# A hybrid attention and mLSTM block: ordered runs for the mLSTM's numerators, later scores, wider first values, and a convolution tap on ScalarE

## The chip, the cores and the metric

The kernel runs on one core of a Trainium2 chip. The metric is device time in microseconds of one execution: 1467.97 us before, the median of 3 runs (1467.61 to 1468.28).

## The reference, cut to what matters

The model has two layers over 512 tokens of width 1024: a dilated window attention and a SwiGLU, then an mLSTM and a SwiGLU, with RMS norms. The change lies in the mLSTM alone. For it the reference computes, with 8 heads, keys and queries of 64 and values of 128:

```
proj = xn @ w_in                      # q, k (512 + 512), v (1024), output gate (1024), gates (16)
qk   = silu(causal depthwise conv over 4 taps of the first 1024 columns, + bias)
dmat = cumsum(log f) differences + i, causal
sm   = exp(dmat - m_t) * (q @ k^T)
num  = sm @ v (+ the carried state);  den = sum of sm
h    = num / max(|den|, exp(-m_t));   h = rms_norm(h) * head_gain
out  = (h * sigmoid(o_pre)) @ w_out
```

The kernel doesn't carry a state between chunks of 64 tokens; it takes all 512 tokens at once, in blocks of 128 by 128 below the diagonal.

## The kernel before, in words

Products are made in split precision: every operand is split into a high and a low part of a rounded fp32 format, and three products (high by high, high by low, low by high: `SPLITS`) stand for one. Weights come in chunks of 128 x 1024 numbers (512 KB) on SyncE's (SP's) DMA queue, with three buffers; for each chunk ScalarE makes the high part (L207) and VectorE the low part (L208). So all projections are long rows of TensorE products, fed by the two other engines.

Two kinds of projection matter here. `project` (L238) has the weights stationary and 512 tokens moving, 512 columns in each product: q and k ("mqk"), the output gate ("mo"), the output projection ("mwo"). `project_tokens` (L270) has tokens stationary and weights moving, 256 columns in each product: the values ("mv"), because the numerators need them by token. `project_v(pr)` makes the values of two heads in two chunks of 48 products, and ScalarE copies them out of PSUM into `vaug` with a scale (L914).

**Ticks.** `advance()` is called after every chunk and counts one tick; `defer` and `at_tick` queue a function for a tick counted from the mLSTM's start. Ticks 1 to 4 follow the four chunks of `project_v(0)` and `project_v(1)`; after tick 2 come the gates (a long chain of small VectorE steps). Ticks 5 to 12 are the eight chunks of q and k (24 products each; the order of the four parts is 0, 2, 1, 3), 13 to 16 those of `project_v(2)` and `project_v(3)`, 17 to 24 those of the output gate. After each part of q and k, `convolve` makes two channels' tiles: VectorE multiplies the first tap (L899), adds three more (L901), and ScalarE applies Silu (L903).

**Per head.** `stack(p)` builds split keys and queries of two heads (L1033 to L1039). `weights(hh)` broadcasts a row into the PSUM tile "nb" (L1049), adds the causal mask (L1051), takes exponentials on ScalarE (L1057, L1060), makes the scores ("m0s" for head 0, L1062 and L1063, eight products in the two "s" banks), and multiplies both on VectorE (L1064). `numerators(hh)` makes ten fp32 products (twenty instructions, L1076) into two tiles of the two "o" banks, takes the denominators and norms (L1084 to L1094, with four squares on ScalarE, L1090), and writes the normalised head `yt` with four VectorE instructions (L1097), two from each bank. `outputs(hh)` transposes `yt` by four TensorE products (L281) in the single "t" bank, which "nb" uses too, and ScalarE copies the result to `y[hh]` (L1106). `HEAD_AT` gives each head its ticks for the three.

**Order.** A tick only sets where a function stands in the program's order. A scheduler then orders each engine's instructions by when it reckons them ready, with the program's order as priority; a TensorE product of a later chunk may overtake a numerator that isn't ready. The engines keep that order on the chip. Two helpers bind it: `run(*fns)` makes all TensorE instructions of the functions follow the last TensorE instruction of the program so far, and notes the run's last one; and a block under `fenced()`, which every projection uses, follows the last run. The attention uses `run` already; in the mLSTM nothing does.

PSUM has eight banks: three "acc", two "s", two "o" and one "t".

Of the kernel before, what the change touches and what calls it, by code (L numbers as in the profile page):

```python
# [11 lines left out]
F32 = mybir.dt.float32  # L12
F32R = mybir.dt.float32r
I32 = mybir.dt.int32
AF = mybir.ActivationFunctionType
ALU = mybir.AluOpType
AX = mybir.AxisListType
P = 128

SEQ = 512  # L20
D = 1024
KC = D // P
TB = SEQ // P
# [11 lines left out]
RUN_AT = (2, 3, 5, 10)  # L35
LAST_AT = (2, 4)
STACK_AT = (9, 11, 14, 16)
HEAD_AT = ((9, 11, 13), (10, 13, 15), (12, 15, 17), (13, 16, 18), (15, 18, 19), (16, 19, 21), (18, 21, 22), (19, 21, 23))
W_BUFS = 3
SPLITS = [(0, 0), (0, 1), (1, 0)]  # L40

# [28 lines left out]
def tile_hybrid_dilated_attn_mlstm(  # L70
# [4 lines left out]
    nc = tc.nc  # L75
# [53 lines left out]
    def col(key, i):  # L129
        return cols[:, row_of[key] + i:row_of[key] + i + 1]  # L130
# [10 lines left out]
    def advance():  # L141
        tick[0] += 1
        run_deferred(lambda t: t <= tick[0])
# [32 lines left out]
    def fenced():  # L176
        return tc.issue_after(fence[0]) if fence[0] is not None else nullcontext()
# [82 lines left out]
    def project_tokens(pairs, w2d, c0, evac, name, tok=lambda t, tb: t[:, tb * P:(tb + 1) * P]):  # L260

        acc = [acc_tile("%s_%d" % (name, m)) for m in range(2)]
        for ch in range(KC // 4):
            whl = split_chunk(weight_chunk(w2d, ch, c0, 4, "%s_k%d" % (name, ch)))
            for m in range(2):
                with fenced():
                    for i, k in itertools.product(range(2), range(4)):
                        kk = ch * 4 + k
                        for a, b in SPLITS:
                            nc.tensor.matmul(  # L270
                                acc[m][:, i * 256:(i + 1) * 256],
                                tok(pairs[a][kk], 2 * m + i), whl[b][:, k, :],
                                start=(kk == 0 and i == 0 and (a, b) == SPLITS[0]),
                                stop=(kk == KC - 1 and (a, b) == SPLITS[-1]),
                                skip_group_check=True)
                if ch == KC // 4 - 1:
                    evac(m, acc[m])
            advance()

    def transpose_into(dst_ps, i, src, n=P):  # L280
# [593 lines left out]
    with ExitStack() as mctx:  # L874
# [20 lines left out]
        def convolve(c):  # L895
            for m in range(2):
                j = 2 * c + m
                u = mp.tile([P, SEQ], F32, tag="conv", name="conv%d" % j, bufs=2)
                nc.vector.tensor_scalar(u, pre[m][:, 0:SEQ], col("convw", j), None, op0=ALU.mult)  # L899
                for w in range(1, 4):  # L900
                    nc.vector.scalar_tensor_tensor(u, pre[m][:, w:w + SEQ], col("convw", w * KC + j), u,  # L901
                                                   op0=ALU.mult, op1=ALU.add)
                nc.scalar.activation(qk[j], u, AF.Silu, bias=col("convb", j))  # L903
# [6 lines left out]
        def project_v(pr):  # L910
            def evac(m, acc):
                for i in range(2):
                    tb = 2 * m + i
                    nc.scalar.activation(  # L914
                        vaug[:, tb, 2 * pr:2 * pr + 2, 0:P],
                        acc[:, i * 256:(i + 1) * 256].rearrange("p (h d) -> p h d", h=2),
                        AF.Copy, scale=rtok[:, tb:tb + 1])
            project_tokens(pair, w_in2, D + pr * 256, evac, "mv%d" % pr)
# [37 lines left out]
        mneg = mp.tile([P, SEQ], F32R, name="mneg")  # L956
        nc.gpsimd.memset(mneg.bitcast(F32), 0.0)
        base = tick[0]
        project_v(0)
        gates()  # L960
        hook()
        ve = nc.vector
# [39 lines left out]
        i = 0  # L1002
# [16 lines left out]
                nc.tensor.transpose(tp[:, i * H:(i + 1) * H], emn[:, b * P:(b + 1) * P], ident[:H, :H])  # L1019
            nc.vector.tensor_copy(bcol.rearrange("p a b -> p (a b)"), tp[:, :(npair + TB) * H])  # L1020

        project_v(1)

        stacks = {}

# [19 lines left out]
        def weights(hh):  # L1045
            nm = "m%d" % hh
            ks, qs, ql = stacks[hh]
            nb = ps.tile([P, 512], F32, tag="t", name=nm + "nb", bufs=1)
            nc.tensor.matmul(nb, sel[:, hh, :], mneg, start=True, stop=True)  # L1049
            tmp = mp.tile([P, TB, P], F32, tag="dtmp", name=nm + "d", bufs=2)  # L1050
            nc.vector.tensor_tensor(tmp, blk(nb), mask_causal_t.unsqueeze(1).to_broadcast([P, TB, P]), op=ALU.add)  # L1051
            sm = []
            for kb in range(TB):
                w = SEQ - kb * P
                e = mp.tile([P, w], F32, tag="e%d" % kb, name=nm + "e", bufs=2)
                bias = lambda qb: bcol[:, pidx[kb, qb], hh:hh + 1]
                nc.scalar.activation(e[:, :P], tmp[:, kb, :], AF.Exp, bias=bias(kb))  # L1057
                for qb in range(kb + 1, TB):
                    o = (qb - kb) * P
                    nc.scalar.activation(e[:, o:o + P], nb[:, qb * P:(qb + 1) * P], AF.Exp, bias=bias(qb))  # L1060
                sp = ps.tile([P, 512], F32, tag="s", name=nm + "s", bufs=2)
                nc.tensor.matmul(sp[:, :w], ks[:, kb * P:(kb + 1) * P], qs[:, kb * P:], start=True, stop=False)  # L1062
                nc.tensor.matmul(sp[:, :w], ks[:, kb * P:(kb + 1) * P], ql[:, kb * P:], start=False, stop=True)  # L1063
                nc.vector.scalar_tensor_tensor(e, sp[:, :w], 0.125, e, op0=ALU.mult, op1=ALU.mult)  # L1064
                sm.append(e)
            sms[hh] = sm

        def numerators(hh):
            nm = "m%d" % hh
            sm = sms[hh]  # L1070
            num = [ps.tile([P, 512], F32, tag="o", name=nm + "num", bufs=2) for _ in range(2)]
            nv = lambda qb: num[qb // 2][:, (qb % 2) * 256:(qb % 2) * 256 + P + 1]
            for qb in range(TB):
                for kb in range(qb + 1):
                    o = (qb - kb) * P
                    nc.tensor.matmul(nv(qb), sm[kb][:, o:o + P], vaug[:, kb, hh, :],  # L1076
                                     start=(kb == 0), stop=(kb == qb))

            rr = mp.tile([P, TB], F32, tag="rr", name=nm + "rr", bufs=2)
            aa = mp.tile([P, TB], F32, tag="aa", name=nm + "aa", bufs=2)  # L1080
            s2 = mp.tile([P, TB], F32, tag="s2", name=nm + "s2", bufs=2)
            for t in range(2):
                den = num[t].rearrange("p (a b) -> p a b", a=2)[:, :, P]
                nc.vector.tensor_copy(rr[:, 2 * t:2 * t + 2], den)  # L1084
            nc.vector.scalar_tensor_tensor(aa, rr, -1.0, rr, op0=ALU.mult, op1=ALU.max)
            nc.vector.tensor_tensor(aa, aa, bcol[:, npair:, hh], op=ALU.max)
            nc.vector.reciprocal(rr, aa)
            for qb in range(TB):
                junk = mp.tile([P, P], F32, tag="junk", name=nm + "j", bufs=2)
                nc.scalar.activation(junk, nv(qb)[:, :P], AF.Square, scale=rr[:, qb:qb + 1],  # L1090
                                     accum_out=s2[:, qb:qb + 1])
            nc.vector.tensor_scalar(s2, s2, 1.0 / P, EPS, op0=ALU.mult, op1=ALU.add)
            rq = rsqrt_newton(mp, s2, TB, nm + "rq")
            nc.vector.tensor_tensor(rr, rr, rq, op=ALU.mult)  # L1094
            yt = mp.tile([P, SEQ], F32, tag="yt", name=nm + "yt", bufs=2)
            for qb in range(TB):
                nc.vector.tensor_scalar(yt[:, qb * P:(qb + 1) * P], nv(qb)[:, :P], rr[:, qb:qb + 1], None,  # L1097
                                        op0=ALU.mult)
            yts[hh] = yt

        def outputs(hh):
            tp = ps.tile([P, 512], F32, tag="t", name="m%dyT" % hh, bufs=1)
            for qb in range(TB):
                transpose_into(tp, qb, yts[hh][:, qb * P:(qb + 1) * P])
            y[hh] = y_tile(hh, "y%d" % hh)
            nc.scalar.activation(y[hh], tp, AF.Copy)  # L1106

        def at_tick(t, fn):
            defer(base + t - tick[0], fn)
        at_tick(8, exponents)  # L1110
        for p, t in enumerate(STACK_AT):
            at_tick(t, lambda p=p: stack(p))
        for hh, (t0_, t1_, t2_) in enumerate(HEAD_AT):
            at_tick(t0_, lambda hh=hh: weights(hh))
            at_tick(t1_, lambda hh=hh: numerators(hh))
            at_tick(t2_, lambda hh=hh: outputs(hh))
        for c in (0, 2, 1, 3):
            project_qk(c)
            convolve(c)
# [6 lines left out]
        for c in range(KC // 2):  # L1126
            def evac(m, acc, c=c):
                j = 2 * c + m
                t = mp.tile([P, SEQ], F32, tag="conv", name="og%d" % j, bufs=2)
                nc.vector.tensor_tensor(t, acc, rbc, op=ALU.mult)  # L1130
                nc.scalar.activation(t, t, AF.Tanh, scale=0.5)
                nc.vector.scalar_tensor_tensor(y[j], t, 1.0, y[j], op0=ALU.add, op1=ALU.mult)
# [114 lines left out]
```

## Time and profile before

| | |
|---|---|
| median of 3 runs | 1467.97 us (1467.61 to 1468.28) |
| the profiled execution's own time | 1467.84 us |
| its span, from first to last instruction | 1466.1 us, granted TensorE clock 0.999 |
| busy: TensorE (PE), weight loads (PEld) | 1454.4 us, 1239.4 us |
| busy: VectorE (DVE), ScalarE (ACT), GpSimd (POOL) | 784.7 us, 528.5 us, 125.3 us |
| the mLSTM, first value product to first product of the output projection | 873.4 to 1050.1 us |

The profile is of one execution. A row of a timeline has the start in microseconds from the span's start, the length, the engine, the source line, the operation, the tiles written and read, and the shapes; a bracket tells how long the engine was idle before it and which instruction released it. Buffer numbers are left out of names, so "mv" stands for all value projections; "f1j" and "fin" are the last SwiGLU. Matmuls overlap in the pipeline: a 512-column product shows 0.39 us, though the next one starts earlier, so spacings are read from start to start.

### The profile page before, as it was taken

What the parts mean: (1) busy time and instruction counts of PE and PEld (TensorE: products, weight loads), DVE (VectorE), ACT (ScalarE), POOL (GpSimd) and SP (SyncE); (2) the same over time, 40 slices, a digit from 0 to 9 for tenths busy, and PEclk for the clock granted to TensorE, in tenths of its full rate; (3) what the DMA queues carried; (4) which work ended last, traced back from release to release, by engine and by line L of the source; (5) the groups of instructions that cost most, each with busy time, mean ns of one, the idle gap of its engine ahead of it and who ended that gap; (6) DMA issues with size and microseconds to landing.
All of it is one profiled execution on the core that took longest, in us unless ns stands there. A gap on an engine that the chain in (4) does not pass through costs nothing. (4 is left out here: it accounts for less than half of the span.)

```text
span 1466.1 us, 18728 instructions
## 1 busy us (share of the span) xinstructions
PE 1454.4 (99%) x7378; PEld 1239.4 (85%) x7378; DVE 784.7 (54%) x1523; ACT 528.5 (36%) x963; POOL 125.3 (9%) x135
## 2 busy tenths in 40 slices
PE   9999999999999999999999999999999999999998
PEld 7898888889888888888888889798888888888887
DVE  8747556556565554344333348987765344343233
ACT  5342233224225433223322233785543222232223
POOL 1001001001001001111110000100000110110001
PEclk9999999999999999999999999999999999999999
DMA  6226226225235323323322232222332333332231
GB/s 201 87 87 202 73 87 198 73 87 179 88 101 165 101 86 101 98 91 99 101 93 94 94 95 87 80 65 61 98 93 95 101 96 93 99 101 87 86 101 72
DMA packets 131665, 150.17 MB, mean 102 GB/s; under 512 B 6068, under 2 KB 122100, under 8 KB 131576
## 3 DMA queue, kind: packets, MB, share of 16 engines
q1 hardware_dynamic: 126384, 131.55, 28.8%
q0 software_dynamic: 3536, 16.30, 3.6%
q8 instruction: 58, 0.95, 0.3%
q10 hardware_dynamic: 1656, 1.12, 0.2%
q14 instruction: 31, 0.25, 0.1%
HBM read 138.99 MB, written 9.96 MB: 102 GB/s over the span
## 5 line engine op out<-in xcount | busy, mean ns | idle before, releaser
L238 PE MATMUL f1j<-n_h,f1j_h 128*128 128x512 f32 x352 | 137.1, 389 | 0.0
L238 PE MATMUL f0j<-n_h,f0j_h 128*128 128x512 f32 x352 | 137.1, 389 | 0.0
L238 PE MATMUL f0j<-n_h,f0j_l 128*128 128x512 f32 x352 | 137.0, 389 | 0.0
L238 PE MATMUL f1j<-n_h,f1j_l 128*128 128x512 f32 x352 | 137.0, 389 | 0.0
L238 PE MATMUL f0j<-n_l,f0j_h 128*128 128x512 f32 x352 | 136.9, 389 | 0.0
L238 PE MATMUL f1j<-n_l,f1j_h 128*128 128x512 f32 x352 | 136.9, 389 | 0.0
L208 DVE TENSOR_TENSOR f0j_l<-f0j_w,f0j_h 128x1024 fp32r<-128x1024 f32 x44 | 54.9, 1247 | 54.8 <-ACT f0j_h L207 54.8
L208 DVE TENSOR_TENSOR f1j_l<-f1j_w,f1j_h 128x1024 fp32r<-128x1024 f32 x44 | 54.8, 1246 | 54.8 <-ACT f1j_h L207 54.8
L238 PEld LDWEIGHTS f1j<-n_h,f1j_l 128*128 128x128 f32 x352 | 66.1, 188 | 13.9
L238 PEld LDWEIGHTS f0j<-n_h,f0j_l 128*128 128x128 f32 x352 | 66.1, 188 | 13.9
L238 PEld LDWEIGHTS f0j<-n_h,f0j_h 128*128 128x128 f32 x352 | 66.1, 188 | 13.8
L238 PEld LDWEIGHTS f1j<-n_l,f1j_h 128*128 128x128 f32 x352 | 66.1, 188 | 13.8
L238 PEld LDWEIGHTS f1j<-n_h,f1j_h 128*128 128x128 f32 x352 | 66.1, 188 | 13.5
L238 PEld LDWEIGHTS f0j<-n_l,f0j_h 128*128 128x128 f32 x352 | 66.1, 188 | 13.5
L207 ACT ACTIVATE f1j_h<-f1j_w 128x1024 fp32r<-128x1024 f32 x44 | 46.5, 1057 | 73.6 <-PE f1j L238 72.5
L207 ACT ACTIVATE f0j_h<-f0j_w 128x1024 fp32r<-128x1024 f32 x44 | 46.5, 1057 | 73.6 <-PE f0j L238 72.5
L1179 PE MATMUL fin<-fw_h,f1ah 128*128 128x512 f32 (+1 forms) x198 | 72.8, 368 | 0.0
L1179 PE MATMUL fin<-fw_l,f1ah 128*128 128x512 f32 (+1 forms) x198 | 72.5, 366 | 0.0
L1179 PE MATMUL fin<-fw_h,f1al 128*128 128x512 f32 (+1 forms) x198 | 72.4, 366 | 0.0
L238 PE MATMUL fo<-f0ah,fo_k_h 128*128 128x512 f32 x176 | 68.5, 389 | 0.0
L238 PE MATMUL fo<-f0al,fo_k_h 128*128 128x512 f32 x176 | 68.5, 389 | 0.0
L238 PE MATMUL fo<-f0ah,fo_k_l 128*128 128x512 f32 x176 | 68.5, 389 | 0.0
(1168 smaller groups left out, 3569.6 us busy)
## 6 DMA issues: line engine op xcount, KB each, us to landing
f0j_w<-in_ffn_w_in_dram SPq DMA_DIRECT2D x44, 512.0 KB, 3.5
f1j_w<-in_ffn_w_in_dram SPq DMA_DIRECT2D x44, 512.0 KB, 3.5
fw_w<-in_ffn_w_out_dram SPq DMA_DIRECT2D x22, 512.0 KB, 3.8
fo_k_w<-in_ffn_w_out_dram SPq DMA_DIRECT2D x20, 512.0 KB, 3.4
awo_k_w<-in_attn_w_out_dram SPq DMA_DIRECT2D x8, 512.0 KB, 4.0
mv_k_w<-in_mlstm_w_in_dram SPq DMA_DIRECT2D x8, 512.0 KB, 3.7
mqk_k_w<-in_mlstm_w_in_dram SPq DMA_DIRECT2D x8, 512.0 KB, 3.6
mo_k_w<-in_mlstm_w_in_dram SPq DMA_DIRECT2D x8, 512.0 KB, 3.7
```

What stands on the lines that cost most here:

```text
L207: nc.scalar.activation(hi[:, :n], raw[:, :n], AF.Copy)
L208: nc.vector.tensor_tensor(lo[:, :n], raw[:, :n], hi[:, :n].bitcast(F32), op=ALU.subtract)
L238: nc.tensor.matmul(acc, whl[a][:, k, m * P:(m + 1) * P], pairs[b][kk], start=(kk == 0 and (a, b) == SPLITS[0]), stop=(kk == nk - 1 and (a, ...
L1179: nc.tensor.matmul(acc[i][:, cs], a[a_][kk][:, tb * P:(tb + 1) * P], whl[b_][:, k, cs], start=(kk == 0 and (a_, b_) == SPLITS[0]), stop=(k ...
```

## The change

Four things are done.

1. The values of the first four heads are made by a new function, `project_tokens_wide`, with 512 columns in each product: four chunks of 24 products instead of four of 48. The chunk holds 256 rows by 512 columns instead of 512 rows by 256. The four accumulators lie in the "s" and "o" banks until the fourth chunk, and are copied to `vaug` by four ScalarE instructions of 512 columns.
2. The first convolution tap goes from VectorE's tensor_scalar to a ScalarE copy with a scale.
3. The scores (`weights`) of heads 0 and 1 come at ticks 10 and 11 instead of 9 and 10; the others stay.
4. Numerators and output transposes go into nine runs. In one tick the run comes first, then the scores. The last head's numerators use the "s" banks and its transpose an "o" bank; `yt` has three buffers instead of two.

The ticks of numerators were 11, 13, 15, 16, 18, 19, 21, 21 for heads 0 to 7 and become 12, 13, 15, 16, 18, 19, 20, 21; those of outputs were 13, 15, 17, 18, 19, 21, 22, 23 and become 15, 16, 18, 19, 21, 21, 23, 23.

```diff
-HEAD_AT = ((9, 11, 13), (10, 13, 15), (12, 15, 17), (13, 16, 18), (15, 18, 19), (16, 19, 21), (18, 21, 22), (19, 21, 23))
+WEIGHTS_AT = (10, 11, 12, 13, 15, 16, 18, 19)
...
+    def project_tokens_wide(pairs, parts, accs, evac, name, chunks=range(KC // 2)):
+        w = 512 // len(parts)
+        for ch in chunks:
+            raw = wp.tile([P, 1024], F32, tag="wraw", name="%s_k%d_w" % (name, ch), bufs=W_BUFS)
+            for i, part in enumerate(parts):
+                nc.sync.dma_start(raw.rearrange("p (k g n) -> p k g n", k=2, n=w)[:, :, i],
+                                  part[2 * ch * P:2 * (ch + 1) * P].rearrange("(k p) n -> p k n", p=P))
+            whl = split_chunk((raw, 1024, lambda t: t.rearrange("p (k n) -> p k n", k=2), "%s_k%d" % (name, ch)))
+            for tb in range(TB):
+                with fenced():
+                    for k in range(2):
+                        kk = 2 * ch + k
+                        for a, b in SPLITS:
+                            nc.tensor.matmul(accs[tb], pairs[a][kk][:, tb * P:(tb + 1) * P], whl[b][:, k, :],
+                                             start=(kk == 0 and (a, b) == SPLITS[0]),
+                                             stop=(kk == KC - 1 and (a, b) == SPLITS[-1]))
+                if ch == KC // 2 - 1:
+                    evac(tb, accs[tb])
+            advance()
...
-                nc.vector.tensor_scalar(u, pre[m][:, 0:SEQ], col("convw", j), None, op0=ALU.mult)
+                nc.scalar.activation(u, pre[m][:, 0:SEQ], AF.Copy, scale=col("convw", j))
...
-        project_v(0)
+        wide = [ps.tile([P, 512], F32, tag=tag, name="mv0", bufs=2) for tag in "soso"]
+
+        def evac_wide(tb, acc):
+            nc.scalar.activation(vaug[:, tb, 0:4, 0:P], acc.rearrange("p (h d) -> p h d", h=4), AF.Copy,
+                                 scale=rtok[:, tb:tb + 1])
+
+        def first_values(chunks):
+            project_tokens_wide(pair, [w_in2[:, D:D + 512]], wide, evac_wide, "mv0", chunks)
+        first_values((0, 1))
...
-        project_v(1)
+        first_values((2, 3))
...
-            num = [ps.tile([P, 512], F32, tag="o", name=nm + "num", bufs=2) for _ in range(2)]
+            num = [ps.tile([P, 512], F32, tag="os"[hh == H - 1], name=nm + "num", bufs=2) for _ in range(2)]
...
-            yt = mp.tile([P, SEQ], F32, tag="yt", name=nm + "yt", bufs=2)
+            yt = mp.tile([P, SEQ], F32, tag="yt", name=nm + "yt", bufs=3)
...
-            tp = ps.tile([P, 512], F32, tag="t", name="m%dyT" % hh, bufs=1)
+            tp = ps.tile([P, 512], F32, tag="to"[hh == H - 1], name="m%dyT" % hh, bufs=1 + (hh == H - 1))
...
-        for hh, (t0_, t1_, t2_) in enumerate(HEAD_AT):
-            at_tick(t0_, lambda hh=hh: weights(hh))
-            at_tick(t1_, lambda hh=hh: numerators(hh))
-            at_tick(t2_, lambda hh=hh: outputs(hh))
+        num, out_ = (lambda hh: lambda: numerators(hh)), (lambda hh: lambda: outputs(hh))
+        for t, fns in ((12, [num(0)]), (13, [num(1)]), (15, [out_(0), num(2)]), (16, [out_(1), num(3)]),
+                       (18, [out_(2), num(4)]), (19, [out_(3), num(5)]), (20, [num(6)]),
+                       (21, [out_(4), num(7), out_(5)]), (23, [out_(6), out_(7)])):
+            at_tick(t, lambda fns=fns: run(*fns))
+        for hh, t in enumerate(WEIGHTS_AT):
+            at_tick(t, lambda hh=hh: weights(hh))
```

## The prediction

> **What bounds the kernel now.** I read the page first, then the windows of the mLSTM stage, then the chain of waits and TensorE's timeline there. On the page, PE is TensorE; each entry gives busy microseconds and the share of the span.
>
> ```profile
> span 1466.1 us, 18728 instructions
> ...
> PE 1454.4 (99%) x7378; PEld 1239.4 (85%) x7378; DVE 784.7 (54%) x1523; ACT 528.5 (36%) x963; POOL 125.3 (9%) x135
> ```
>
> TensorE is busy for 99% of the span, so time is saved only by fewer TensorE microseconds or fewer gaps between its products, and a new gap costs its whole length. The windows of the stage that the diff touches (columns: length, then busy time of PE, PEld, DVE, ACT and POOL, then the granted clock):
>
> ```profile
> 890.80:963.40 72.60, 71.28 (x409) 61.76 (x408) 70.63 (x145) 47.35 (x86) 4.64 (x6) 1.00 0.29 87
> 930.00:938.30 8.30, 6.97 (x31) 5.14 (x29) 8.05 (x12) 8.16 (x18) 0.61 (x1) 1.00 0.23 63
> 938.30:953.70 15.40, 15.40 (x82) 13.22 (x83) 15.27 (x31) 11.61 (x29) 1.75 (x2) 1.00 0.34 102
> 953.70:977.00 23.30, 23.30 (x187) 22.69 (x186) 20.69 (x65) 22.34 (x49) 0.85 (x2) 1.00 0.16 48
> ```
>
> VectorE is full from 890.8 to 963.4 (70.63 of 72.60): it is behind its work, and in 930 to 938.3 TensorE is idle for 1.33 us because of it. ScalarE has room until 953.7 (11.61 of 15.40), but almost none from 953.7 to 977 (22.34 of 23.30). The timeline shows the two waits (start, duration; a start that is late after the one before is the gap; the bracket names the releaser):
>
> ```profile
> 931.35 0.39 PE L238 MATMUL mqk<-n_h,mqk_k_l 128*128 128x512 f32 x1
> 932.41 0.50 PE L1062 MATMUL m0s<-qs,ks 128*128 128x512 f32 x1 [0.67 <-DVE ks L1034]
> 932.75 0.40 PE L1063 MATMUL m0s<-ql,ks 128*128 128x512 f32 x1
> ...
> 937.25 0.39 PE L238 MATMUL mqk<-n_h,mqk_k_l 128*128 128x512 f32 x1
> 938.29 0.39 PE L1062 MATMUL m0s<-qs,ks 128*128 128x256 f32 x1 [0.65 <-DVE m0e L1064]
> 938.51 0.28 PE L1063 MATMUL m0s<-ql,ks 128*128 128x256 f32 x1
> ```
>
> Products overlap, so I count from start to start. The long-run spacing comes from the chain that ended last (start, length, how many in a row):
>
> ```profile
> 948.37 5.46 PE mqk L238 x24
> ...
> 954.89 5.04 PE mv L270 x42
> ```
>
> A 512-column product takes 5.46 / 24 = 227.5 ns, a 256-column one 5.04 / 42 = 120.0 ns. The same view around a later head shows its neighbours (four output transposes, twenty numerator products, then the next head's first scores):
>
> ```profile
> 1002.75 0.44 PE m3yT L281 x4
> 1003.19 2.23 PE m4num L1076 x20
> 1005.42 0.23 PE m6nb L1049
> ...
> 1006.47 0.70 PE mo L238 x3
> ```
> Back in the timeline, head 0's first score thus started 1.06 - 0.23 = 0.83 us late and its third 1.04 - 0.23 = 0.81; each restart also cost about 0.1 (0.34 and 0.22 to the next product, where 0.23 and 0.12 are usual). Together about 1.85 us.
>
> **First values.** 192 products of 256 columns become 96 of 512. By the spacings, 96 x (2 x 120.0 - 227.5) = 1200 ns: **-1.2 us**, nothing covers it, it is taken from the bound engine. Loads stay four of 512 KB on SP's queue in the same places, with longer rows. The Trainium skill, page "TensorE: Matmul & The Clock Gate", section "Back-to-back issue gap", puts isolated spacing at N/2.4 + 2.5 ns; by that estimate the saving would be 96 x (2 x 109.2 - 215.8) = 0.25 us and the whole sum 0.95 us less gain. The trace's 120.0 and 227.5 ns are larger, and pairs of 256 lose more than the rule says; I go by them.
>
> The evacuation becomes four 512-column copies at the end of the fourth chunk, instead of eight half as wide, four of them earlier. The prices on ScalarE, with VectorE's for the convolution tap:
>
> ```profile
> L914 ACT ACTIVATE vaug<-mv,n2r x16: 467/476/549, 883.8 to 987.8; 128x256 f32<-128x256 f32 x16
> ...
> L225 ACT ACTIVATE yo_h<-y,halfgain x8: 712/726/745, 1042.6 to 1054.1; 128x512 fp32r<-128x512 f32 x8
> ...
> L899 DVE TENSOR_SCALAR conv<-pre,cols x8: 472/479/926, 913.8 to 956.5; 128x512 f32<-128x512 f32 x8
> ```
>
> Four at up to 0.73 are 2.9 us at most, before the 192 products of q and k; ScalarE has over 25 us idle between 890.8 and 963.4 (47.35 of 72.60 busy). I cost it at 0; without that cover the next weight split would be up to 2.9 us late. The four accumulators take both "s" and both "o" banks, which nobody wants before the first scores, six chunks later.
>
> **First tap.** Eight tensor_scalars of 0.48 leave VectorE (3.8 us), and eight copies with a scale, of the form of L225, join ScalarE (8 x 0.73 = 5.8 us). No TensorE time changes by itself; the gain is that VectorE is less behind. Six fall before or near 953.7, where ScalarE has 3.8 us free; two fall at its full stretch, if they are late (a rival below).
>
> **Scores one chunk later.** Heads 0 and 1 move by 24 products, 5.5 us; no instruction is added. Before, the keys' halves (L1034) and the first weighting (L1064) were 0.83 and 0.81 us late. Later by 5.5 and with 1.9 us of taps gone from VectorE ahead of them (four taps), both should be ready: between 0 and -1.85, and I take **-1.7**, a small remainder for the exponentials behind ScalarE's table load. Late next would be head 0's numerators, but they move a chunk too.
>
> **Runs: what goes.** Three output transposes were placed before their input was there:
>
> ```profile
> 1012.42 0.40 PE L1062 MATMUL m7s<-qs,ks 128*128 128x512 f32 x1
> 1012.84 0.30 PE L281 MATMUL m4yT<-cst,m4yt 128*128 128x128 f32 x1
> ...
> 1037.07 0.39 PE L238 MATMUL mo<-n_h,mo_k_l 128*128 128x512 f32 x1
> 1037.58 0.30 PE L281 MATMUL m6yT<-cst,m6yt 128*128 128x128 f32 x1
> ...
> 1049.61 0.39 PE L238 MATMUL mo<-n_h,mo_k_l 128*128 128x512 f32 x1
> 1050.06 0.30 PE L281 MATMUL m7yT<-cst,m7yt 128*128 128x128 f32 x1
> 1050.11 0.48 PE L238 MATMUL mwo<-yo_h,mwo_k_h 128*128 128x512 f32 x1
> 1050.43 0.27 PE L281 MATMUL m7yT<-cst,m7yt 128*128 128x128 f32 x1
> ```
>
> Start to start 0.42, 0.51 and 0.45 against 0.23: 0.19 + 0.28 + 0.22 = 0.7 us. The runs put the transposes of heads 4, 6 and 7 two or three chunks behind their numerators: **-0.7**. Changing between fp32 and split products I cost at 0: in the last rows a transpose inside other products takes 0.05 and the next product 0.32, 0.37 together, where 0.44 / 4 + 0.23 = 0.34 is the price apart.
>
> **Runs: what comes.** A run's products start after the chunk before it, and the next chunk's start after its last. Two numerator banks serve all heads but the last. When the next run is one chunk later (runs 13, 16, 19 and 20), its numerators must wait until the head before has been normalised out of the first bank. Before, TensorE went on with projections meanwhile; now 24 or 48 products queue behind the wait, and only the unfenced scores may pass. How long a bank is held (first to last start of a head's numerators, then of its four normalising writes):
>
> ```profile
> L1076 PE MATMUL m0num<-vaug,m0e x20: 271/275/275, 946.0 to 948.1; 128*128 128x129 f32 x20
> ...
> L1076 PE MATMUL m2num<-vaug,m2e x20: 275/275/276, 977.5 to 979.6; 128*128 128x129 f32 x20
> L1076 PE MATMUL m3num<-vaug,m3e x20: 275/275/377, 987.5 to 989.7; 128*128 128x129 f32 x20
> L1076 PE MATMUL m4num<-vaug,m4e x20: 275/275/276, 1003.0 to 1005.1; 128*128 128x129 f32 x20
> L1076 PE MATMUL m5num<-vaug,m5e x20: 275/275/276, 1013.4 to 1015.7; 128*128 128x129 f32 x20
> ```
>
> ```profile
> L1097 DVE TENSOR_SCALAR m0yt<-m0num,m0rr x4: 338/339/343, 962.3 to 963.1; 128x128 f32<-128x128 f32 x4
> ...
> L1097 DVE TENSOR_SCALAR m2yt<-m2num,m2rr x4: 342/343/351, 986.8 to 987.6; 128x128 f32<-128x128 f32 x4
> L1097 DVE TENSOR_SCALAR m3yt<-m3num,m3rr x4: 341/341/351, 996.6 to 997.4; 128x128 f32<-128x128 f32 x4
> L1097 DVE TENSOR_SCALAR m4yt<-m4num,m4rr x4: 343/343/351, 1012.3 to 1013.1; 128x128 f32<-128x128 f32 x4
> L1097 DVE TENSOR_SCALAR m5yt<-m5num,m5rr x4: 343/344/351, 1025.9 to 1026.7; 128x128 f32<-128x128 f32 x4
> ```
>
> From the last numerator's start to the first write: heads 0, 2, 3, 4, 5: 14.2, 7.2, 6.9, 7.2, 10.2 us. The first bank is free after the second write, 0.27 + 0.34 = 0.6 later: 14.8, 7.8, 7.5, 7.8, 10.8. The room for it, from the rows of the chain above, after a run: the last numerator 0.1, the next scores' first part 1006.47 - 1005.42 = 1.05, their rest about 0.4 (an estimate from half and quarter widths of the same products), and a chunk: 24 x 0.2275 = 5.5, or 48 x 0.120 = 5.8 for values. That is 7.4 at run 13, 7.8 at 16 and 7.5 at 19 (both with 0.44 of transposes ahead), 7.1 at 20.
>
> Run 16 (head 2, 7.8, same neighbours as before): 0. Run 19 (head 4, 7.8): 0.2 after rounding down a little for the lighter VectorE. Run 20 (head 5): between 7.5 and 10.8, since output gates and score weightings mix into its chain; nearest is head 4's 7.8, with one gate product of 0.6 that half a chunk of mo makes ready in time: 8.3, so +1.2. Run 13 (head 0): between 7.5 and 14.8. The long row is from a full VectorE; with 3.8 us of taps and 1.2 us of TensorE time gone, VectorE should be nearly level with its work, nearest the 7.8 of head 2, plus some taps of the last convolution: 8.1, so +0.7. Together **+2.1**, with ends 0.1 and 11.
>
> **The sum.** -1.2 - 1.7 - 0.7 + 2.1 = -1.5 us. The profiled execution took 1467.84, close to the median of 1467.97, of which 1.7 lies around the span. Its time becomes 1466.3.
>
> **Rivals.**
> 1. *The chains are in time.* If the lighter VectorE lets all banks go within the room, the new waits come to 0.5 and the sum is -3.6 + 0.5 = -3.1: 1464.7, or 1464.2 if short waits of later scores go too. For it: head 3's 7.5 where VectorE had little else. Against: 7.5 is still over run 20's 7.1. Chance 0.28.
> 2. *The bank wait takes the place of the score wait, and more.* Head 0's chain keeps its 14.8 and head 5's its 10.8; runs 13 and 20 wait 7.4 and 3.7: -3.6 + 11.1 + 0.2 = +7.7, 1475.5; with half of it, 1470 to 1472. It decides for slower once new waits pass 3.6 + 2.9 = 6.5 us. For it: the order of VectorE, where every small step of a chain lets a large one in. Against: those rows come from a full VectorE. Chance 0.14.
> 3. *ScalarE becomes late.* Two taps of 0.73 and one more pair of table loads (1.28 each, below) in 953.7 to 977, where 0.96 us is free, push exponentials 1.5 + 2.6 - 1.0 = 3.1 us back, and a run with them: 1469.4. Chance 0.08.
>
> ```profile
> 934.28 1.28 ACT L1057 ACT_TABLE_LOAD   x1
> ```
>
> The Trainium skill, page "ScalarE: Activation LUTs", section "Rules for kernel authors", says a plain multiplication belongs on VectorE; by this rule the tap loses. The rows agree on price (0.73 against 0.48); the windows say that VectorE is the scarcer one until 963.
>
> 4. *It doesn't do what it says*: scores placed a chunk later are late again, because the program's order lets ScalarE and VectorE take other work first. Then -1.7 falls away: 1468.0. Chance 0.06.
>
> The forecast has the rest, 0.44.
>
> **How the numbers follow.** 0.2% is 2.9 us, about what a measurement can tell from no change. Faster than 1465.0 is nearly all of rival 1 and a little of the forecast's edge: 0.29. Slower than 1470.9 is rival 2: 0.14. Same: 0.57. The likeliest case alone runs from 1465.0 to 1468.0 (waits of 0.8 to 3.8). The range takes in rival 1, 3 and 4 and leaves out most of 2: 1463.9 to 1469.6.
>
> **What would show it.** Right: first values in 21.8 us of products rather than 23.0; no gap above 0.2 us ahead of head 0's scores; a gap ahead of head 6's numerators of about a microsecond and a smaller one ahead of head 1's, released by VectorE's L1097. Wrong: no such gap (rival 1), a gap of 3 us and more ahead of head 1's (2), gaps released by ScalarE (3), or the same gap at m0s (4). A slower clock in these windows, or a gap at the weight loads, would be something I haven't counted.

## The result and the profile after

The changed kernel takes 1475.95 us (median of 4 runs, 1475.81 to 1476.79), against 1467.79 for the kernel before on the same chips (4 runs): a ratio of 1.0057, 95% interval 1.0044 to 1.0071. That is 8.2 us slower, where 1466.3 was predicted. The profiled execution took 1476.79 us, the longest of the four, so its own balance (+8.95 against 1467.84) is a little larger than that of the medians.

In the new source the lines have moved: scores are L1094 and L1095, their weighting L1096, numerators L1108, the normalised head L1129, transposes L304, the value products L270 (256 columns) and L296 (512).

The page, for the whole kernel:

```profile
span 1475.0 us, 18537 instructions
...
PE 1456.7 (99%) x7282; PEld 1237.5 (84%) x7282; DVE 783.9 (53%) x1515; ACT 535.0 (36%) x969; POOL 124.9 (8%) x135
```

TensorE has 96 instructions less and still 2.3 us more busy time (1454.4 before): some of its products must have become slower. The rest of the added span is idle time. The list of TensorE's waits (engine, waiting product, releaser: total, times, longest) says where:

```profile
PE m6num L1108 <- DVE m5yt L1129: 3.7, 1, 3.7
PE m0s L1094 <- DVE m0e L1096: 2.1, 1, 2.1
PE m2s L1094 <- DVE m2e L1096: 2.1, 1, 2.1
```

Before, the mLSTM's largest waits were the two of head 0's scores. The timeline gives the places, start to start:

```profile
940.18 0.39 PE L238 MATMUL mqk<-n_h,mqk_k_h 128*128 128x512 f32 x1
942.66 0.39 PE L1094 MATMUL m0s<-qs,ks 128*128 128x256 f32 x1 [2.09 <-DVE m0e L1096]
...
959.98 0.28 PE L270 MATMUL mv<-mv_k_h,n_l 128*128 128x256 f32 x1
962.35 0.49 PE L1094 MATMUL m2s<-qs,ks 128*128 128x256 f32 x1 [2.09 <-DVE m2e L1096]
...
1025.70 0.39 PE L238 MATMUL mo<-n_h,mo_k_l 128*128 128x512 f32 x1
1029.75 1.57 PE L1108 MATMUL m6num<-vaug,m6e 128*128 128x129 f32 x10 [3.66 <-DVE m5yt L1129]
```

By spacing they cost 2.48 - 0.23 = 2.25, 2.37 - 0.12 = 2.25 and 4.05 - 0.23 = 3.82 us. The windows around them (length, busy time of PE, PEld, DVE, ACT and POOL, then the granted clock) add what the waits don't show:

```profile
951.10:962.40 11.30, 9.21 (x75) 8.88 (x73) 10.96 (x29) 11.12 (x27) 2.23 (x2) 1.00 0.16 47
962.40:968.00 5.60, 5.60 (x29) 4.79 (x30) 4.46 (x14) 5.50 (x8) 0.00 (x0) 0.70 0.01 3
1018.70:1029.70 11.00, 7.38 (x36) 5.63 (x34) 8.61 (x30) 6.39 (x21) 0.00 (x0) 1.00 0.19 54
1029.70:1033.20 3.50, 3.45 (x21) 3.48 (x21) 0.58 (x3) 0.00 (x0) 0.00 (x0) 0.65 0.39 136
```

Over these windows behind the second and the third wait the granted clock is 0.70 and 0.65 on average. In finer windows it is 0.50 from 962.5 to 965.8 and from 1030.8 to 1034.1 us, which loses about 1.7 us each time; slow numerators are spaced 214 ns instead of 112. Run 20's twenty numerators, right behind the third wait, take 3.4 us instead of 2.2.

Put together, from the first value product to the first output product the stage grew from 176.7 to 185.9 us. By start-to-start spacings: first values -1.2; head 0's scores +0.6 (2.25 for 1.65); head 2's third score +2.25; slow products behind it and head 1's bank wait together +1.8; head 5's numerators +0.25; head 6's bank wait +3.8; slow products behind it +1.7; short waits of transposes -0.7. That is +8.5 of +9.2; I haven't placed the remainder.

### The profile page after: what moved, and what is told of

The parts are those of the page before. It is cut to its first block, busy times and chain, and to the rows that moved or that the text cites. A ratio compares the mean times of both kernels' runs of the same rounds, so it can differ in the third digit from the quotient of the medians.

```text
span 1475.0 us, 18537 instructions
## 1 busy us (share of the span) xinstructions
PE 1456.7 (99%) x7282; PEld 1237.5 (84%) x7282; DVE 783.9 (53%) x1515; ACT 535.0 (36%) x969; POOL 124.9 (8%) x135
```

## The experiments

The theory after the result: **the runs make the loss** (a bank that VectorE gives back late becomes a wait of TensorE), and what the other three parts save is handed back at the next wait that VectorE or ScalarE releases. The rival: each part loses something by itself, ScalarE's new taps above all. Times are medians; the kernel before had 1467.7 to 1468.0 beside them.

### One part at a time

`wide_alone` has only the first values with 512 columns.

> Only the 512-column first values, on the kernel before. My step: 96 x (2 x 120.0 - 227.5) ns = -1.2 us, so 1466.6 beside 1467.8, and the products of the first values in 21.8 us instead of 23.0. Rival: the four accumulators or the later copies hold something up; then it gains less than 0.6 us or loses.

1467.92 us, ratio 1.0000 (0.9990 to 1.0009). The products did save: from the first value product to the first of q and k 26.8 us instead of 28.0. But head 0's scores then waited 1.06 and 1.35 us instead of 0.83 and 0.81, and head 2's third 0.37: together about as much as was saved.

`tap_alone` moves the first convolution tap:

```diff
-                nc.vector.tensor_scalar(u, pre[m][:, 0:SEQ], col("convw", j), None, op0=ALU.mult)
+                nc.scalar.activation(u, pre[m][:, 0:SEQ], AF.Copy, scale=col("convw", j))
```

> Only the first convolution tap on ScalarE. Theory S (ScalarE is late and reloads its tables more often): +1 to +4 us, with waits of head 0's and head 2's scores for an exponential of 1 to 2 us each and two more table loads between 905 and 966 us than before (7 instead of 5). Theory V (VectorE was the late one, as predicted): -0.5 to -1.9 us, the two waits of head 0's scores get shorter.

1469.37 us, ratio 1.0011 (1.0002 to 1.0021): a loss, not 0. Head 0's first score waits 1.9 us for the keys instead of 0.83. The Trainium skill's rule, page "ScalarE: Activation LUTs", section "Rules for kernel authors", that a plain multiplication belongs on VectorE, holds here for the part by itself.

`later_alone` moves the scores of heads 0 and 1:

```diff
-HEAD_AT = ((9, 11, 13), (10, 13, 15), ...
+HEAD_AT = ((10, 11, 13), (11, 13, 15), ...
```

> Only the scores of heads 0 and 1 one chunk later. As predicted: -1.2 to -1.9 us, no wait ahead of head 0's scores. Rival: the wait only moves, since the exponentials come later as well (their table load lands among the convolutions): -0.5 to +1.5 us with a wait of 1 to 2 us at head 0's third score.

1468.39 us, ratio 1.0003 (0.9994 to 1.0013). The first score no longer waits; the third waits 1.22 us for head 0's first weighting, and head 3's third 1.06. The wait only changed its place.

`runs_alone` has the nine runs and their banks, with the scores at the old ticks (`WEIGHTS_AT = (9, 10, 12, ...)`).

> Only the nine runs, with the scores at their old ticks. Theory R (the bank wait): head 5's chain does not depend on the other parts, so the wait of 3.8 us ahead of head 6's numerators and the slow clock after it (2.2 us) stay; with waits for head 0's chain of 1 to 7 us at the second run, and 0.7 us of short waits gone: +6 to +12 us. Rival: the runs cost little by themselves (0 to +2 us) and the waits come from ScalarE and VectorE being late through the tap and the later scores.

1482.24 us, ratio 1.0098 (1.0083 to 1.0113): 14.3 us slower, more than either theory had. Its waits:

```profile
PE m1num L1076 <- DVE m0yt L1097: 7.1, 1, 7.1
PE m6num L1076 <- DVE m5yt L1097: 3.7, 1, 3.7
```

Behind them the numerators are slow: head 1's twenty take 4.5 us, at half the clock.

```profile
L1076 PE MATMUL m1num<-vaug,m1e x20: 422/422/554, 969.0 to 973.3; 128*128 128x129 f32 x20
```
```profile
969.00:973.50 4.50, 4.46 (x21) 4.49 (x22) 0.57 (x3) 0.40 (x1) 0.00 (x0) 0.50 0.00 0
```

These are the two waits of the second rival, 7.4 and 3.7, close by (7.25 and 3.82 from start to start). So the runs alone lose more than the whole change; something in the other three parts takes some 6 us off.

### All but one

`all_but_runs` has the three others, `all_but_tap` everything except the tap.

> The three other parts together, numerators and transposes unbound as before. If the parts add up (0.0 + 1.4 + 0.4): 1469.8. If they help each other as the prediction had it (the wait of head 0's scores gone, the saved products kept): 1465 to 1466. If the waits of 2.2 us at head 0's and at head 2's scores in the changed kernel are theirs and not the runs': 1469 to 1471.

1467.80 us, ratio 1.0001 (0.9992 to 1.0010): without the runs nothing is lost, and nothing gained, which lies in none of my three ranges. The profile shows a wait of 2.27 us at head 0's third score and slow products behind it:

```profile
PE m0s L1094 <- DVE m0e L1096: 2.1, 1, 2.1
```
```profile
942.70:946.60 3.90, 3.90 (x23) 3.90 (x22) 2.39 (x5) 3.85 (x7) 0.00 (x0) 0.56 0.37 125
```

The wait is 0.6 us more than the two score waits before, and the list of waits has 0.4 and 0.2 us more at head 3's broadcast and at one of its scores: together the 1.2 us that the first values save. The slow products don't belong to the median. The profiled execution is the longest of ten, 1468.81 us at a granted clock of 0.998; the other nine took 1467.60 to 1468.21 us at 0.999.

> The changed kernel with the first tap back on VectorE. If the tap is what shortens head 0's chain (7.2 us wait at the second run in the runs alone, 1 to 2 here): VectorE is full again, the wait comes back, 1480 to 1482 us. Rival: the tap costs here what it costs alone (1.4 us), and the time falls to 1474 to 1475.

1476.10 us, ratio 1.0056 (1.0041 to 1.0071), by its median the same as the changed kernel. But its four runs stand in two groups, 1474.83 and 1475.07 at a granted clock of 0.997 and 0.998, 1477.12 and 1477.55 at 0.995, so what the tap costs here isn't resolved. I had expected head 1's wait of 7 us to come back with the taps on VectorE. It didn't (0.85): it isn't the tap that shortens it.

### Which part shortens head 1's wait

`later_runs` has runs and later scores, `wide_runs` runs and wide values, neither has the tap.

> The runs and the scores one chunk later (as in the changed kernel), without the wide values and the tap. Theory that head 0's numerators' chain on VectorE and ScalarE is queued behind the scores and taps of the same chunks, so that with the scores later it meets fewer of them: head 1's numerators wait about 1 us instead of 7.2, head 6's still 3.7, time about 1477 us. Rival, it is the wide values that do it: wait about 7, time 1481 to 1483 us.

> The runs and the wide first values, with the scores at their old chunks and the tap on VectorE. Theory that the later scores shorten the wait of head 1's numerators: here it stays at 6 to 8 us, time 1481 to 1483 us. Rival, the wide values do it: wait about 1 us, time about 1476 us.

1476.80 us (1.0062, 1.0047 to 1.0077) and 1477.03 us (1.0067, 1.0052 to 1.0082). Head 1's numerators wait 0.84 us in the first and 1.44 in the second: **either part alone does it**, so both theories, one part each, were wrong. VectorE's timeline shows the larger part of why. In `runs_alone` this is head 0's normalising chain (small steps of 0.15 us, m0rq):

```profile
960.72 0.16 DVE L188 TENSOR_SCALAR m0rq_y<-m0rq_a 128x4 int32<-128x4 int32 x1
960.79 1.22 DVE L208 TENSOR_TENSOR mv_k_l<-mv_k_w,mv_k_h 128x1024 fp32r<-128x1024 f32 x1
961.92 0.15 DVE L190 SCALAR_TENSOR_TENSOR m0rq_a<-m0rq_y 128x4 f32<-128x4 f32 x1
962.00 0.68 DVE L1051 TENSOR_TENSOR m3d<-m3nb,cst 128x512 f32<-128x512 f32 x1
962.60 0.15 DVE L191 TENSOR_TENSOR m0rq_a<-m0rq_a,m0s 128x4 f32<-128x4 f32 x1
962.78 0.69 DVE L1034 TENSOR_TENSOR ks<-mqk,ks 64x512 fp32r<-64x512 f32 x1
...
968.28 0.35 DVE L1097 TENSOR_SCALAR m0yt<-m0num,m0rr 128x128 f32<-128x128 f32 x1
```

and the same steps in `later_runs`:

```profile
959.86 0.17 DVE L188 TENSOR_SCALAR m0rq_y<-m0rq_a 128x4 int32<-128x4 int32 x1
960.07 0.16 DVE L190 SCALAR_TENSOR_TENSOR m0rq_a<-m0rq_y 128x4 f32<-128x4 f32 x1
960.26 0.16 DVE L191 TENSOR_TENSOR m0rq_a<-m0rq_a,m0s 128x4 f32<-128x4 f32 x1
...
963.76 0.61 DVE L1097 TENSOR_SCALAR m0yt<-m0num,m0rr 128x128 f32<-128x128 f32 x2
```

The steps are the same; what stands between them isn't. In the first, a large instruction stands behind nearly every small one, 7.6 us from the second step to the first write; in the second several small ones follow each other, 3.9 us. By starts, the time from head 0's last numerator to head 1's first falls from 15.2 us in `runs_alone` to 11.8 in `later_runs` and 11.3 in `wide_runs`: 3.4 and 3.9 of the 6.4 and 5.8 us by which the wait shrinks. The rest is TensorE's: it has 7.9 us of other products and waits in between in `runs_alone`, 10.9 and 9.9 in the others, among them head 2's score wait of 1.53 us in `later_runs`. The order on VectorE is fixed before the kernel runs, and each of these edits reshuffles it. How long a bank is held is thus no property of the head, and can't be carried from one kernel's profile to another's.

### Taking the bank wait away

`other_bank` gives the "s" banks to head 6's numerators instead of head 7's:

```diff
-tag="os"[hh == H - 1], name=nm + "num"
+tag="os"[hh == H - 2], name=nm + "num"
```

> The changed kernel, with head 6's numerators in the two s banks and head 7's in the two o banks, so that run 20 need not wait for head 5's chain. Theory R: the wait of 3.8 us ahead of head 6's numerators goes, and with it the slow products after it (2.2 us, clock 0.65): about 1476.0 - 6.0 = 1470.0 us. Rival: something else is late there (the scores or the weights of head 7) and the time moves less than 2 us.

1471.72 us, ratio 1.0026 (1.0016 to 1.0036): 4.2 us of the 8.2 are gone, and so is head 6's wait. That is less than the theory's 6.0 and more than its rival's 2. The two score waits of 2.25 us are still there, and so is a slow clock behind head 2's, in this profile over all of head 1's numerators:

```profile
964.20:969.00 4.80, 4.79 (x26) 4.80 (x27) 2.78 (x8) 4.27 (x7) 0.00 (x0) 0.64 0.00 0
```

`warm_wait` keeps the wait, but fills it with 16 products that nobody reads, 512 columns each, ahead of head 6's numerators in run 20.

> The changed kernel, with 16 idle 512-column products ahead of head 6's numerators in run 20, into the t bank; they compute nothing that is used. They fill about 3.6 us of the 3.8 us wait. Theory K (the slow products after the wait come from the clock, which falls when TensorE stands still): the clock stays at 1.00 and 2 us are gained, 1474.0. Rival: head 6's numerators are slow because their inputs or the banks come slowly: no gain, 1476.0 or more.

The windows of the two kernels, same length, from the start of head 6's numerators: 21 products at a clock of 0.65 before (above), and with the filling

```profile
1029.80:1033.30 3.50, 3.50 (x26) 3.28 (x26) 1.28 (x7) 0.08 (x1) 0.00 (x0) 1.00 0.41 137
```

So the idle time itself makes the slow products; in all five profiles that have this wait of 3.8 us unfilled (the changed kernel, `runs_alone`, `all_but_tap`, `later_runs`, `wide_runs`) the clock is 0.50 to 0.65 over the 3.5 us behind it. But the median is 1475.62 (1.0054, 1.0037 to 1.0071), 0.3 below the changed kernel. The two profiled spans differ by 1.5, but one is of the longest of four executions and the other of the shortest: the gain in time is not resolved by these runs.

### Taking the score waits away

Head 0's third score waits because both "s" banks hold scores that VectorE has yet to weight. The two numerator banks are free then:

```diff
-                sp = ps.tile([P, 512], F32, tag="s", name=nm + "s", bufs=2)
+                sp = ps.tile([P, 512], F32, tag="so"[hh == 0 and kb > 1], name=nm + "s", bufs=2)
```

Two kernels have this beside the other edits without runs (`abc_spare`: all three; `wide_later_spare`: without the tap; in both, head 0's numerators come at tick 12), two beside the runs and the bank of `other_bank` (`mended`, and `mended_no_tap` without the tap).

> First values wide, tap on ScalarE, scores one chunk later, as in the kernel with all but the runs (1467.80 us), but head 0's third and fourth scores take the two banks that the numerators will use and that are free until then, so the third score needs no earlier weighting; head 0's numerators go in one chunk later so that they don't meet the same wait. Theory that the bank wait of head 0's third score (2.27 us) and the 15 slow products behind it (about 1.9 us) are what eats the gain of the three edits: 1467.8 - 2.3 - 1.9 = about 1463.7 us, 1463 to 1465. Rival that the time is bounded by the VectorE and ScalarE chains of the later heads there: a longer wait turns up at head 2's or head 3's scores or at the first output transposes, and the time stays at 1467 to 1468.

> The same without the first tap on ScalarE (VectorE keeps it). The tap alone cost 1.4 us. Theory that ScalarE's table loads and the taps were the price: head 0's score waits go (they were 0.9 and 1.35 us with the wide values alone, of which the first needs the scores later and the second the spare banks), 1467.9 - 2.2 = about 1465.7 us, and below the kernel with the tap if the tap costs more than the 0.5 us or so that VectorE gets from it. Rival, the waits move to head 2's or head 3's scores: 1467 to 1468.

> The changed kernel (1475.95 us) with its two bank waits taken away by other banks: head 6's numerators in the score banks instead of head 7's (1471.72 us by itself), and head 0's third and fourth scores in the free numerator banks. Theory: 1471.7 - 2.25 (the wait at head 0's third score) - 0 to 2 (slow products) = 1467.5 to 1469.5 us, with head 2's third score still waiting 2.2 us and head 1's numerators at the slow clock behind it. Rival, head 0's wait is only passed on to head 2's third score or head 1's numerators: 1471 to 1472 us.

> The same without the first tap on ScalarE, so the kernel with all but the tap (1476.10 us) with both bank changes. Theory: 1476.1 - 3.7 (head 6's numerators) - 2.2 (their slow products) - 1.7 (head 0's third score) = about 1468.5 us, with the 1.4 us at head 2's third score and 0.7 at head 1's numerators left; below the kernel with the tap by up to 1 us. Rival, passed on: 1471 to 1472 us.

1469.20 (1.0010, 1.0000 to 1.0019), 1467.57 (0.9998, 0.9989 to 1.0008), 1471.38 (1.0023, 1.0014 to 1.0033) and 1469.58 us (1.0013, 1.0004 to 1.0023). The wait at head 0's third score is gone in all four, but little of it came back as time: `abc_spare` is even above its rival's range, `wide_later_spare` and `mended` lie in theirs, `mended_no_tap` between the two. (The 1.9 us of slow products that I had hoped to win in `abc_spare` weren't in the median it started from.) Here the tap shows a price: 1.6 us between the first two kernels, whose ten runs each don't overlap, and 1.8 us by medians between the last two. In `abc_spare` waits of 0.94, 1.20 and 1.29 us turned up at head 1's broadcast, head 1's third score and head 2's. The start of head 1's numerators is the same too: 963.4 us in the kernel before, 963.6 in both kernels without runs. In the kernel before, VectorE is busy for 11.87 of 12.00 and 17.19 of 17.40 us up to there, which would explain it:

```profile
934.00:946.00 12.00, 11.35 (x54) 9.13 (x54) 11.87 (x22) 10.16 (x26) 0.61 (x1) 1.00 0.01 3
946.00:963.40 17.40, 17.40 (x119) 16.05 (x118) 17.19 (x45) 14.82 (x31) 1.75 (x2) 1.00 0.41 122
```

That VectorE sets this start is argued and not shown: in `later_alone`, `all_but_runs` and `tap_alone` head 1's numerators start at 961.1 to 961.8 us, and these kernels aren't faster (1468.39, 1467.80 and 1469.37 us).

`spare_alone` puts only this into the kernel before, `wide_spare` adds the wide values, both with scores and numerators at their old ticks.

> The kernel before with head 0's third and fourth scores in the two numerator banks, nothing else. The wait of 0.81 us at the third score goes. Theory that VectorE (11.87 of 12.0 us busy from 934 to 946 us, 17.19 of 17.4 to 963.4) sets when head 1's numerators can start: they start at 963.4 us as before, 1467.5 to 1468 us. Rival, TensorE's wait counts: 1467.0 us.

> The same with the wide first values, scores at their old chunks. Theory of the bound by VectorE: head 1's numerators start at about 963.5 us again, waits turn up at later scores, 1467.3 to 1468 us. Rival, TensorE's waits count: 1467.9 - 1.35 = about 1466.5 us, below the kernel before.

1467.73 (0.9998, 0.9989 to 1.0007) and 1467.14 us (0.9995, 0.9986 to 1.0004), with 1468.0 before beside them. Head 1's numerators started at 963.6 and 962.5. The second is between the two theories: 0.9 us lower by medians and by spans (1465.2 against 1466.1), though the interval doesn't exclude no change. It is the best kernel of the study, 8.8 us below the changed one.

### The tap on a third engine

If VectorE is the bound and ScalarE's queue the objection, GpSimd, idle for most of the stage, could take the tap:

```diff
-                nc.vector.tensor_scalar(u, pre[m][:, 0:SEQ], col("convw", j), None, op0=ALU.mult)
+                nc.gpsimd.tensor_scalar(u, pre[m][:, 0:SEQ], col("convw", j), None, op0=ALU.mult)
```

> The kernel before with the first convolution tap on GpSimd: 8 instructions of 0.479 us off VectorE, as with the tap on ScalarE (1469.4 us), but ScalarE gets none. Theory that VectorE's and ScalarE's queues bound 930 to 963 us: head 0's score waits (1.65 us) shrink, 1466.5 to 1467.9 us, and below the tap on ScalarE by 1.5 us or more. Rival, that GpSimd's slower taps (1.2 to 1.7 us by its 128x512 additions and multiplications elsewhere) lengthen each convolution and the scores wait for the stacks instead: 1469 to 1471 us.

> First values wide, scores one chunk later, first tap on GpSimd, the old order of numerators. Theory that VectorE's queue was what kept these edits from paying: 1465 to 1466.5 us, which is below both kernels. Rival, ScalarE's queue (table loads, copies, exponentials) bounds that stretch as much, and the wait at head 0's third score stays near 2 us: 1467.5 to 1468.5 us.

1476.56 (1.0060, 1.0043 to 1.0076) and 1478.12 us (1.0069, 1.0054 to 1.0084). Theory and rival both missed, by 6 to 12 us: the tap takes 1.57 us on GpSimd, VectorE waits for it six times, and head 0's scores wait for the keys in `pool_tap`:

```profile
DVE conv L901 <- POOL conv L899: 5.9, 6, 1.7
```
```profile
PE m0s L1062 <- DVE ks L1034: 5.5, 1, 5.5
```

VectorE has less to do (24.97 us busy from 905 to 936.6 us, where the kernel before has 30.64) and is still later. Its own instructions aren't slower: the taps that it keeps take 0.746 us beside the 0.742 before. The slow clock adds to the loss, 0.50 over the 3.5 us behind the wait for the keys. It is the chain's latency through the engines, not the sum of VectorE's work alone, that the scores wait for.

## Why the prediction was wrong, step by step

Three steps failed: the -1.7 for the scores, the hold of head 5's bank within the +2.1 of the runs, and the clock behind a wait, which the sum put at nothing. Term by term:

- **First values, -1.2.** Right as a term (26.8 us for the part that took 28.0), wrong as time: by itself it is worth 0.0 (interval -1.5 to +1.3 us), because the next product to wait for VectorE waits longer. "Nothing covers it, it is taken from the bound engine" was the fault: TensorE is the bound of the kernel, but ahead of head 0's scores it waits for VectorE, and what it saves there it waits longer.
- **Scores one chunk later, -1.7.** Failed, and by size the furthest off. The keys were ready, but the third score also needs a bank that the first weighting frees, and that moved along: 2.25 us instead of 1.65 in the changed kernel, and 2.25 more at head 2. It is what the fourth rival had named, scores that are late again because ScalarE and VectorE take other work first, at a chance of 0.06. VectorE's timeline in the changed kernel shows what stood ahead of the first weighting (L1096), after the mask at 937.5:

```profile
938.14 2.73 DVE L924 SCALAR_TENSOR_TENSOR conv<-pre,cols,conv 128x512 f32<-128x512 f32 x4
940.79 1.22 DVE L208 TENSOR_TENSOR mv_k_l<-mv_k_w,mv_k_h 128x1024 fp32r<-128x1024 f32 x1
941.92 1.15 DVE L1096 SCALAR_TENSOR_TENSOR m0e<-m0s,m0e 128x512 f32<-128x512 f32 x2
```

  A "small remainder" was my word for that; four taps and a weight split are 3.8 us. They aren't all of the wait. ScalarE's exponentials for the first weighting end at 940.9 us, behind a table load:

```profile
938.40 1.28 ACT L1089 ACT_TABLE_LOAD   x1
939.70 0.40 ACT L1089 ACTIVATE m0e<-m0d,bcol 128x128 f32<-128x128 f32 x1
940.01 0.86 ACT L1092 ACTIVATE m0e<-m0nb,bcol 128x128 f32<-128x128 f32 x3
```

  So of the wait, which runs from 940.4 to 942.7, about 0.5 us are still ScalarE's, 1.0 are VectorE's other work, and 0.7 are the weighting itself.
- **First tap, 0.** By itself +1.4, and 1.6 to 1.8 where the bank waits are gone. In the changed kernel its share isn't resolved (1476.10 without, in two groups of runs, 1475.95 with it). It takes part in head 2's wait: 1.54 without it, 2.25 with. The third rival had the place right: ScalarE is busy 11.12 of 11.30 us ahead of that score, and its order there shows two table loads before the exponentials can begin:

```profile
955.18 1.28 ACT L926 ACT_TABLE_LOAD   x1
956.48 0.72 ACT L926 ACTIVATE mqk<-conv,cols 128x512 f32<-128x512 f32 x1
957.11 0.35 ACT L1122 ACTIVATE m0j<-m0num,m0rr 128x128 f32<-128x128 f32 x1
...
958.61 1.28 ACT L1089 ACT_TABLE_LOAD   x1
959.91 0.40 ACT L1089 ACTIVATE m2e<-m2d,bcol 128x128 f32<-128x128 f32 x1
```

  Head 0's squares (m0j) stand in this place with its numerators at tick 12 and its scores at 10; with numerators at 11 (`all_but_runs`) or scores at 9 (`runs_alone`, `wide_runs`) head 2's score doesn't wait for them. `abc_spare` fits too: it has no runs, but numerators at 12 and scores at 10, and that score waits 1.29 us. No run tests this reading by itself.
- **Short waits of transposes, -0.7.** Right.
- **Runs, +2.1.** Right in mechanism: bank waits released by L1129, at head 1 and head 6, none at head 3. Head 1: +0.7 forecast, and in the changed kernel the load ahead of its numerators waits 0.7 us for L1129, part of it under slow products. That is luck: head 0's bank was held for 11.6 us, not 8.1, and head 2's score wait took up most of the difference. Head 5: 0.2 forecast, 0.25 measured. **Head 6: +1.2 forecast, 3.8 measured. This is the step whose removal gives back most** (`other_bank`, 4.2 of 8.2 us). I took 8.3 us for head 5's hold, from head 4's 7.8 and one gate product (7.8 and 0.6 are 8.4), where the row of head 5 itself said 10.2 and 10.8. The timeline of the changed kernel shows the chain with a large instruction after almost every small one:

```profile
1024.00 0.15 DVE L192 SCALAR_TENSOR_TENSOR m5rq_y<-m5rq_a,m5rq_y 128x4 f32<-128x4 f32 x1
1024.07 0.55 DVE L1096 SCALAR_TENSOR_TENSOR m7e<-m7s,m7e 128x384 f32<-128x384 f32 x1
1024.54 0.15 DVE L190 SCALAR_TENSOR_TENSOR m5rq_a<-m5rq_y 128x4 f32<-128x4 f32 x1
...
1025.01 0.68 DVE L1168 SCALAR_TENSOR_TENSOR y<-og,y 128x512 f32<-128x512 f32 x1
...
1026.98 1.23 DVE L208 TENSOR_TENSOR mo_k_l<-mo_k_w,mo_k_h 128x1024 fp32r<-128x1024 f32 x1
...
1028.99 1.13 DVE L1129 TENSOR_SCALAR m5yt<-m5num,m5rr 128x128 f32<-128x128 f32 x4
```

  Four instructions for two gates (2.7 us), four weightings of head 7 (1.9) and one weight split (1.2) lie in it. Head 4's chain in the kernel before has four weightings too (1.9), but no gate and no split; so the addition to its 7.8 was 3.9 us of instructions, where I put 0.6. The same four and the split already stood in head 5's chain before:

```profile
1019.33 0.69 DVE L1130 TENSOR_TENSOR og<-mo,n2rbc 128x512 f32<-128x512 f32 x1
...
1021.87 0.68 DVE L1132 SCALAR_TENSOR_TENSOR y<-og,y 128x512 f32<-128x512 f32 x1
...
1023.48 1.22 DVE L208 TENSOR_TENSOR mo_k_l<-mo_k_w,mo_k_h 128x1024 fp32r<-128x1024 f32 x1
```

  The hold is 1029.0 - 1018.7 + 0.6 = 10.9; less the room of 7.1 that is the 3.8.
- **The clock**, named as uncounted, is about 3 us in the profiled execution: the slow products behind two waits. The prediction had new waits cost their length alone. With it, the size of the second rival (1475.5) is right for a partly other reason: its 3.7 at head 6 came as 3.8, its 7.4 at head 1 didn't come, and head 2's wait and the slow clock stood in for it.

## What to carry to other kernels

An ordered run turns a late result, around which the scheduler used to reorder, into a wait of its full length: price it with the longest hold that the profile shows at that very place, not with a kinder neighbour. Time saved on the busiest engine counts only if the next product that waits for another engine would have been ready earlier too; look for it before counting the saving. And where a small chain shares an engine with large instructions, its length is set by what the schedule puts between its steps, so that any edit nearby may halve or double it.

## What the hardware did that I had not expected

An idle stretch of 2.25 us can be enough to lose TensorE's clock, and it comes back late. In fine windows the granted clock is 1.00 or 0.50, and at 0.50 numerators come every 214 ns instead of 112. The slow stretches behind waits of about 2 us last 3.3 to 3.4 us, so they lose about 1.7 us each. They can begin late: in the changed kernel the clock is still 0.90 over the first 1.3 us behind head 6's wait. Behind the longest wait, 7.25 us in `runs_alone`, products ran at 0.50 from 969.0 to 975.0 us, which loses 3.0. The waits of 0.8 us in the kernel before cost little beside themselves.

It isn't sure at 2.25: in the profiles here five of eight such waits are followed by a slow stretch within 3 us, two of them after one more short wait, and in the changed kernel the one at head 2 is and the one at head 0 isn't. In `wide_later_pool` a wait of 1.95 us was enough, in `tap_alone` one of 1.92 wasn't. All eight waits of 3.8 us and more in this stage that nothing filled were followed by one. The Trainium skill, page "TensorE: Matmul & The Clock Gate", section "Part 1: The HAM clock gate", has half rate after an idle window of about 3.4 us that runs freely. The half rate agrees with these traces (0.50). A dependence on phase would fit them, since waits of one length differ in what follows, but no run here varies the phase by itself. Waits of 2.25 us, shorter than that window, were enough in several places. By these runs, the price of a wait of 2 us or more is its length and, where the clock falls, 1.7 to 3 us on top.
